# Decoder step with sparse and forgetting heads: two buffers for the compression's prompt rows, both turns behind the second group's loads, and products with cached value pages given out a little later

## The chip, the cores and the metric

The kernel runs on one core of one Trainium2 chip. A core has a matrix engine (TensorE, PE in the profile, with its weight loads as PEld), a vector engine (VectorE, DVE), a scalar engine (ScalarE, ACT), a general engine (GpSimd, POOL) and a sync engine (SyncE, SP). Each runs its own list of instructions in order; they meet at semaphores. SP and POOL also give out DMA transfers. The metric is the device time of one execution in microseconds (us); less is better.

## The reference

One layer of a decoder on two groups of tokens that share all weights: a prompt of 512 tokens, and 8 samples of 4 tokens, each with a past of 1024 tokens in a paged cache (8 pages of 128 rows, found through a page table). Model width 2048, 16 heads of width 128, all in float32.

```python
h = rmsnorm(x, norm_in)
q_n, kv_n, g_n, z_n, q_f, k_f, v_f, f_f, z_f = split(h @ w_in)      # 7712 columns
# 8 sparse heads, 2 shared key/value heads
kc = compress(kv_n[0], cmp_pe[0], cmp_w[0])   # blocks of 32 rows -> one row, 32 products of 128x128
vc = compress(kv_n[1], cmp_pe[1], cmp_w[1])
o_n = g0 * attend(q_n, kc, vc) + g1 * attend(q_n, top 16 blocks of 64) + g2 * attend(q_n, window 512)
# 8 forgetting heads
o_f = softmax(q_f k_f^T / sqrt(128) + D[t] - D[s]) v_f,  D = cumsum(log sigmoid(f_f))
y = rmsnorm(x + concat(o_n * silu(z_n), o_f * silu(z_f)) @ w_out, norm_final)
```

For the samples, keys and values of the past come from the caches, so the kernel reads whole pages of `cache_nsa_kv` and `cache_fox_kv`, and the window from `state_nsa_win`. The compression works on the prompt's rows and on the cached rows of all samples. The new keys, values and log forget values, and the window moved on, are outputs too.

## The kernel before

**A planner writes the order.** The kernel is a Python program that gives out instructions once. A model of the chip (`Clock`, `note` at L105) keeps a time for each engine and DMA queue. The input projection runs as 61 tiles of 128 columns (`run_tiles`, L519): each of four chunks of a tile is 24 matmuls of 272 columns into `pz` (three products for each pair of 128x272 blocks: high by high, high by low, low by high part). Between these matmuls, `S.pump` (L223) lets generators go on that do all other work. A generator yields what it waits for: a list of tiles (until the model has them ready), flags, or a test. `S.after(us)` (L270) is a test that holds until the model's PE clock has gone that far. None of these becomes an instruction; they only move what the generator gives out next, in the order of every engine. The real waits are semaphores that follow the data. All engine calls go through one helper, so that the profile has the line L169 for all, and work is told apart by the names of tiles.

**Weights.** A chunk's weights (`raw`, five buffers, 256 KB from SP) are split into a high part on ACT (`whi`) and a low part on DVE (`wlo`), two chunks ahead of the products (`w_dma` L469, `w_split` L494).

**Compression** (`compress`, L1246). For keys and values (kv = 0 and 1) it first needs the prompt's rows of the tiles c00 and c01, and of c10 and c11. They have just been stored by `store_natural` (L731), which raises the flags nkv00 to nkv11. Eight loads on SP bring the rows of one kv back as `cz`, 64 KB each, in runs of 512 bytes; DVE turns them into `more`, 8 us on the planner's clock after `cz` is ready there. Then come 64 steps with rows gathered from the cache (`crow`, POOL), ending in the results `vt`, `kc_scr` and `vc_scr`.

**The sparse chain** (`nsa`, L2087) runs compression, the prompt's sparse heads (`nsa_prompt`, two halves, the second waits for the flags nkv31 and nkv51 among others) and the samples' sparse heads (`nsa_sample`, L1553). The last has, for each of two groups of four samples, six pairs of value pages: `set_in` (L1569) keeps five page buffers `spg` filled, half of the pages through SP and half through POOL, and `values` (L1806) gives 16 matmuls into `acc` for each pair of two. When this chain ends the flag mx is raised, and the mixing begins.

**The forgetting chain** (`fox`, L2102) runs twice, for four heads each: samples (`fox_sample`, L1084), then prompt (`fox_prompt`, last step `fot`). In the samples' value part a step takes two pages `fpg` of four samples each (eight loads of 256 KB, half on SP and half on POOL), 16 matmuls into `accv`, and asks for the next pages behind them (`ahead`, L1092, two buffers). There are 8 steps in each half, 16 in all.

**The end.** `mix` (L1852) loads for each of 16 heads the gate (`mx`) and the result (`oz`) and multiplies them on DVE; `turn_in` (L1868) splits that into `h_hi` and `h_lo`, and `run_outputs` (L593) multiplies with `w_out` into `po`, head after head.

Of the kernel before, what the change touches and what calls it, by code (L numbers as in the profile page):

```python
# [8 lines left out]
F32 = mybir.dt.float32  # L9
# [6 lines left out]
P = 128  # L16
# [283 lines left out]
def dram(ap, offset, dims):  # L300
    return bass.AP(tensor=ap.tensor, offset=ap.offset + offset, ap=dims)
# [3 lines left out]
def trunk_step(ctx, tc, x_prompt, x_sample, cache_nsa_kv, cache_fox_kv, cache_fox_logf, state_nsa_win,  # L305
# [25 lines left out]
    S = Streams(clock)  # L331
# [44 lines left out]
    def tr_tile(shape, name="tr"):  # L376
        return psum.tile(shape, F32, name=name, tag="tr", bufs=2)
# [4 lines left out]
    def cp(out, in_, scale=1.0):  # L382
        nc.scalar.activation(out, in_, AF.Copy, scale=scale)
# [19 lines left out]
    def mm(out, a, b, start=True, stop=True):  # L403
        nc.tensor.matmul(out, a, b, start=start, stop=stop, skip_group_check=True)
# [361 lines left out]
    def post_qn(h):  # L766
        def f(zt):
            nc.sync.dma_start(z_scr[h], zt)
            flags.add(f"nq{h}")
            yield  # L770
        return f
# [23 lines left out]
    def post_vf(h):  # L795
        def f(zt):
            yield from store_natural(zt, *dst_fox(h, 1), True, f"v{h}")
        return f
# [72 lines left out]
    def load(t, src):  # L871
        nc.sync.dma_start(t, src)
        return t
# [210 lines left out]
    def fox_sample(hh):  # L1084
# [7 lines left out]
        def ahead():  # L1092
            while at[0] < min(len(seq), at[1] + FPG):
                kv, bq, kb = seq[at[0]]
                pages[at[0]] = pg = fx.tile([P, 4, 512], F32, name="fpg", bufs=FPG)
                for b in range(4):
                    if kv:
                        load_page(pg[:, b], cache_fox_kv, (bq * 4 + b) * 8 + kb,
                                  lambda c: c[0, :, 1, hs, :].rearrange("p h d -> p (h d)"))
                    else:  # L1100
                        gather(pg[:, b], dram(cache_fox_kv, 0, [[512, n_pool * 512], [1, 512]]),
                               IX["f"][hh][:, bq * 8 + kb, b:b + 1])
                at[0] += 1
# [100 lines left out]
        for bq in range(2):  # L1204
            acc = psum.tile([P, SEQ], F32, name="accv", tag="accv", bufs=1)
            for kp in range(4):
                pgs = [pages.pop(at[1] + x) for x in range(2)]
                yield [*pgs, pt, acc]
                for x in range(2):
                    kb = kp * 2 + x  # L1210
                    for b in range(4):
                        o = kb * P + (bq * 4 + b) * 16
                        mm(acc[b * 32:b * 32 + 32], pt[:, o:o + 32], pgs[x][:, b], kb == 0, kb == 7)
                at[1] += 2
                yield
                ahead()
            ob = obs[bq]
            cp(ob, acc)
            yield
            yield from S.take()  # L1220
            tp = tr_tile([P, 4, P])
            for g in range(4):
                nc.tensor.transpose(tp[:, g, :], ob[:, g * P:(g + 1) * P], ident)
            yield
            for g in range(4):
                nc.vector.tensor_copy(o_s[:, 8 + hh * 4 + g, bq * 16:bq * 16 + 16].rearrange("p (b t) -> p b t", t=4),
                                      tp[:, g, :].rearrange("p (b r) -> p b r", r=32)[:, :, g * 4:g * 4 + 4])
            S.put()
# [17 lines left out]
    def compress(pl):  # L1246
# [17 lines left out]
        def load_w(s):  # L1264
            if s < 32:
                cg, kv, dp = s // 4, s // 2 % 2, s % 2
                cw[s] = t = pl.tile([P, 2, P], F32, name="cw", bufs=3)
                for d in range(2):
                    load(t[:, d], dram(cmp_w, (kv * 32 + cg * 4) * P * P + (dp * 2 + d) * 32 * P, [[P * P, 4], [P, 32], [1, P]]))
        load_rows(0)  # L1270
        load_w(0)
        load_w(1)
        more = []
        for kv in range(2):
            yield (f"nkv{kv}0", f"nkv{kv}1")
            yield [dram(nsa_kv_prompt, kv * 256 + v * P, [[1024, SEQ], [1, P]]) for v in range(2)]
            cz = pl.tile([P, 8, P], F32, name="cz")
            for c in range(4):
                for v in range(2):
                    load(cz[c * 32 + v * 16:c * 32 + v * 16 + 16],  # L1280
                         dram(nsa_kv_prompt, kv * 256 + v * P + c * 1024, [[32 * 1024, 16], [4 * 1024, 8], [1, P]]))
            yield [cz]
            yield S.after(8.0)
            m = pl.tile([P, 32, MORE], F32, name=f"more{kv}")
            more.append(m)
            nc.vector.memset(m[:, :, 33:], 0.0)
            nc.vector.tensor_copy(m.rearrange("p (g d) k -> p g d k", d=4)[:, :, :, 32],
                                  peT[:, :, kv * 8:kv * 8 + 8].rearrange("p d g -> p g d"))
            nc.vector.transpose(m[:, :, :32], cz.rearrange("p g d -> p (g d)"))
            yield  # L1290
# [12 lines left out]
        for step in steps + [None]:  # L1303
            if step:
                cg, bh, kv, dp = step
# [6 lines left out]
                n = 256 if bh else WIDE  # L1312
# [19 lines left out]
        for kv in range(2):  # L1332
            bc = pl.tile([P, 1], F32, name="bc", bufs=2)
            nc.vector.tensor_copy(bc, pss[kv][:, 288:289])
            pc = pl.tile([P, 32], F32, name="pc", bufs=2)
            nc.vector.tensor_scalar(pc, pss[kv][:, 256:288], bc, None, op0=OP.add)
            vt = pl.tile([P, 2, 8, 32], F32, name="vt", bufs=2)
            for bh in range(2):
                src = (psb[:, kv] if bh else pss[kv][:, :256]).rearrange("p (b v n) -> p v b n", b=4, v=2)
                for v in range(2):  # L1340
                    nc.scalar.activation(vt[:, v, bh * 4:bh * 4 + 4], src[:, v], AF.Identity, bias=bc)
            yield
            vf = vt.rearrange("p v b n -> p v (b n)")
            if kv == 0:
                nc.sync.dma_start(kp_scr, pc)
                nc.sync.dma_start(kc_scr, vf)
            else:
                yield from S.take(2)
                tp = tr_tile([P, 2, 256])
                for grp in range(2):  # L1350
                    for v in range(2):
                        nc.tensor.transpose(tp[:, grp, v * P:(v + 1) * P], vf[:, v, grp * P:(grp + 1) * P], ident)
                tq = tr_tile([16, 2, P])
                for v in range(2):
                    nc.tensor.transpose(tq[:, v, :], pc[:, v * 16:(v + 1) * 16], ident)
                yield
                vn = pl.tile([P, 2, 256], F32, name="crow", bufs=2)
                cp(vn, tp)
                vq = pl.tile([P, 2, P], F32, name="cw", bufs=3)[:16]
                cp(vq, tq)  # L1360
                S.put(2)
                yield
                nc.sync.dma_start(vc_scr, vn)
                nc.sync.dma_start(vp_scr, vq)
# [188 lines left out]
    def nsa_sample(pl):  # L1553
# [82 lines left out]
        for grp in range(2):  # L1636
# [14 lines left out]
            for x in range(2):  # L1651
                a, b = slice(64 * x, 64 * x + 64), slice(64 - 64 * x, 128 - 64 * x)
# [66 lines left out]
            for br in range(2):  # L1719
# [34 lines left out]
                p = T("sp", [P, 1024 + 64]) if br == 0 else p  # L1754
# [51 lines left out]
            def values(k, srcs, n=P, first=False, last=False):  # L1806
                for bb in range(4):
                    mm(acc[bb * 32:bb * 32 + 32], PT[:n, k, bb * 32:bb * 32 + 32], srcs[bb], first, last)
            yield [acc, PT]
            for k in range(0, 12, 2):  # L1810
                ts = [got.pop(0) for _ in range(2)]
                yield ts + [vc] * (k == 8)
                if k == 8:
                    values(12, [vs] * 4, 64)
                    values(13, [vc[:, grp, :]] * 4)
                for x in range(2):
                    values(k + x, [ts[x][:, bb] for bb in range(4)], first=k + x == 0, last=k + x == 11)
                yield ts
                set_in()
                set_in()  # L1820
# [82 lines left out]
    def add_in(col, post):  # L1903
        add_tile(w_in2, [(col, P, 0)], post)
# [3 lines left out]
                 n=lambda h, _: add_in(C_QN + h * P, post_qn(h)),  # L1908
                 q=lambda h, _: add_in(C_QF + h * P, post_qf(h)),
                 k=lambda h, _: add_in(C_KF + h * P, post_kf(h)),  # L1910
                 v=lambda h, _: add_in(C_VF + h * P, post_vf(h)),
# [243 lines left out]
```

## Time and profile before

| what | value |
|---|---|
| median of 3 runs | 1295.4 us (1294.78 to 1297.54) |
| profiled execution, its own time | 1292.8 us |
| its span, first to last instruction | 1291.1 us |
| mean granted clock of TensorE | 0.993 |
| DMA | 266.86 MB, mean 207 GB/s |

The page of the profile gives the busy time of each engine, the span in 40 slices, the DMA queues, the chain of work that ended last, and the costliest groups. The views used further on are the waits (who waited for whom: total, times, longest), the timeline (start, length, engine, line, operation, out<-in, in brackets the idle time before and what ended it), the table by windows (busy time and instructions of each engine in a stretch, the granted clock of PE, the busy share of the DMA engines, GB/s) and the groups of one tile. Times of the trace are of the one profiled execution. Matmuls overlap: the length of one is longer than the step to the next, so a start is the safer thing to read.

### The profile page before, as it was taken

What the parts mean: (1) busy time and instruction counts of PE and PEld (TensorE: products, weight loads), DVE (VectorE), ACT (ScalarE), POOL (GpSimd) and SP (SyncE); (2) the same over time, 40 slices, a digit from 0 to 9 for tenths busy, and PEclk for the clock granted to TensorE, in tenths of its full rate; (3) what the DMA queues carried; (4) which work ended last, traced back from release to release, by engine and by line L of the source; (5) the groups of instructions that cost most, each with busy time, mean ns of one, the idle gap of its engine ahead of it and who ended that gap; (6) DMA issues with size and microseconds to landing.
All of it is one profiled execution on the core that took longest, in us unless ns stands there. A gap on an engine that the chain in (4) does not pass through costs nothing.

```text
span 1291.1 us, 27195 instructions
## 1 busy us (share of the span) xinstructions
PE 1254.9 (97%) x10071; PEld 1130.4 (88%) x10071; DVE 784.5 (61%) x1978; ACT 549.8 (43%) x1193; POOL 284.5 (22%) x376
## 2 busy tenths in 40 slices
PE   8989999999999999999999999899999999999997
PEld 6989999998789999999998888688889988777786
DVE  6735888885546667655687753386566537354255
ACT  5313333434334677652345452256754524333221
POOL 5221277753410000005445012211111200000000
PEclk9989999999999999999999999999999999999999
DMA  7476699998986455659967688977788697334323
GB/s 214 129 192 170 178 279 298 299 288 272 295 272 160 121 157 155 174 157 292 294 199 235 174 239 244 257 211 198 217 233 202 196 304 258 100 114 147 127 76 139
DMA packets 308398, 266.86 MB, mean 207 GB/s; under 512 B 87198, under 2 KB 255150, under 8 KB 307592
## 3 DMA queue, kind: packets, MB, share of 16 engines
q1 hardware_dynamic: 284312, 189.15, 51.4%
q0 software_dynamic: 23904, 75.84, 18.3%
q8 instruction: 79, 1.29, 0.4%
q14 instruction: 55, 0.45, 0.1%
q10 hardware_dynamic: 48, 0.13, 0.0%
HBM read 236.32 MB, written 37.05 MB: 212 GB/s over the span
## 4 chain that ended last, share of the span: by engine, by line
PE 73%; DMA 10%; issue 9%; POOL 2%; DVE 2%; SPq 2%; ACT 2%; POOLq 0%; DVEq 0%; ACTq 0%
PE pz L169 40%; PE po L169 15%; DMA fpg<-in_cache_fox_kv 4%; PE tr L169 4%; PE accv L169 4%; PE s L169 4%; PE acc L169 3%; SPq L169 2%; DMA spg<-in_cache_nsa_kv 1%; POOL crow L169 1%; PE psb L169 1%; DMA spg<-in_state_nsa_win 1%; PE accf L169 1%; DMA xt<-in_x_prompt 1%; POOL fpg L169 1%
## 5 line engine op out<-in xcount | busy, mean ns | idle before, releaser
L169 PE MATMUL pz<-h_hi,whi 128*128 128x272 f32 x1920 | 565.6, 295 | 2.2 <-DVE zt L169 1.6
L169 PE MATMUL pz<-h_hi,wlo 128*128 128x272 f32 x1920 | 554.9, 289 | 5.8 <-DVE wlo L169 5.8
L169 PE MATMUL pz<-h_lo,whi 128*128 128x272 f32 x1920 | 554.4, 289 | 0.0
L169 PEld LDWEIGHTS pz<-h_hi,whi 128*128 128x128 f32 x1920 | 363.4, 189 | 18.2 <-issue 13.6
L169 PEld LDWEIGHTS pz<-h_hi,wlo 128*128 128x128 f32 x1920 | 362.8, 189 | 6.0 <-DVE wlo L169 6.0
L169 PEld LDWEIGHTS pz<-h_lo,whi 128*128 128x128 f32 x1920 | 363.3, 189 | 0.8
L169 DVE TENSOR_TENSOR wlo<-raw,whi 128x512 fp32r<-128x512 f32 x275 | 186.0, 678 | 157.7 <-ACT whi L169 152.9
L169 ACT ACTIVATE whi<-raw 128x512 fp32r<-128x512 f32 x275 | 171.5, 625 | 210.4 <-PE pz L169 96.9
L169 POOL DMA_INDIRECT fpg<-in_cache_fox_kv,fi x128 | 131.6, 1028 | 300.4 <-ACT whi L169 209.7
L169 PE MATMUL po<-whi,h_hi 128*128 128x512 f32 (+1 forms) x256 | 95.5, 373 | 0.0
L169 POOL DMA_INDIRECT crow<-in_cache_nsa_kv,ci x64 | 66.0, 1031 | 125.6 <-DVE ct L169 71.8
L169 PE MATMUL po<-whi,h_lo 128*128 128x512 f32 (+1 forms) x256 | 93.4, 365 | 0.0
L169 PE MATMUL po<-wlo,h_hi 128*128 128x512 f32 (+1 forms) x256 | 93.4, 365 | 0.0
L169 DVE STREAM_TRANSPOSE ft<-fpg 128x1024 f32<-128x1024 f32 x64 | 78.9, 1235 | 17.3 <-DMA fpg<-in_cache_fox_kv,fi 13.2
L169 ACT ACTIVATE cxh<-ct 128x580 fp32r<-128x580 f32 (+1 forms) x64 | 42.2, 660 | 85.1 <-DVE ct L169 75.2
L169 DVE TENSOR_TENSOR zt<-pz,rsb 128x272 f32<-128x272 f32 x56 | 24.6, 439 | 85.3 <-PE pz L169 85.3
L169 POOL DMA_DIRECT2D spg<-in_cache_nsa_kv x64 | 35.0, 546 | 185.3 <-DVE skt L169 57.6
L169 ACT ACTIVATE zt<-pz 128x272 f32<-128x272 f32 x66 | 26.2, 398 | 98.7 <-PE pz L169 98.5
L169 PEld LDWEIGHTS po<-whi,h_hi 128*128 128x128 f32 x256 | 48.1, 188 | 19.7 <-ACT whi L169 7.5
L169 POOL DMA_DIRECT2D fpg<-in_cache_fox_kv x64 | 34.8, 544 | 133.8 <-PE accv L169 96.0
L169 DVE TENSOR_TENSOR cxl<-ct,cxh 128x580 fp32r<-128x580 f32 (+1 forms) x64 | 46.1, 720 | 19.4 <-ACT cxh L169 18.6
L169 PEld LDWEIGHTS po<-whi,h_lo 128*128 128x128 f32 x256 | 48.2, 188 | 8.5
(409 smaller groups left out, 1907.1 us busy)
## 6 DMA issues: line engine op xcount, KB each, us to landing
raw<-in_w_in SPq DMA_DIRECT2D x240, 256.0 KB
fpg<-in_cache_fox_kv POOLq DMA_DIRECT2D x64, 256.0 KB, 7.0
fpg<-in_cache_fox_kv SPq DMA_DIRECT2D x64, 256.0 KB
raw<-in_w_out SPq DMA_DIRECT2D x40, 256.0 KB
spg<-in_cache_nsa_kv POOLq DMA_DIRECT2D x64, 128.0 KB, 5.4
spg<-in_cache_nsa_kv SPq DMA_DIRECT2D x64, 128.0 KB
out<-in_state_nsa_win SPq DMA_DIRECT2D x32, 254.0 KB
scr_z<-zt SPq DMA_DIRECT2D x28, 272.0 KB
```

The source lines that it names most:

```text
L169: return fn(*a, **k)
```

## The change

It has two parts.

In `compress`, the loop over kv is cut in two. The first loop waits for the flags, takes a buffer `cz` and gives out its eight loads; `cz` now has two buffers. The second loop does the two turns into `more`, each 8 us after the buffer is ready on the planner's clock. `vt` at the end takes the two slots of `cz` in place of its own.

In `fox_sample` and in `nsa_sample`, each step of products with value pages yields `S.after(1.5)` once the planner has the pages ready: 16 steps into `accv`, 12 into `acc`.

```diff
@@ fox_sample @@
                 pgs = [pages.pop(at[1] + x) for x in range(2)]
                 yield [*pgs, pt, acc]
+                yield S.after(1.5)
                 for x in range(2):
@@ compress @@
-        more = []
+        more, czs = [], []
         for kv in range(2):
             yield (f"nkv{kv}0", f"nkv{kv}1")
             yield [dram(nsa_kv_prompt, kv * 256 + v * P, [[1024, SEQ], [1, P]]) for v in range(2)]
-            cz = pl.tile([P, 8, P], F32, name="cz")
+            czs.append(pl.tile([P, 8, P], F32, name="cz", bufs=2))
             for c in range(4):
                 for v in range(2):
-                    load(cz[c * 32 + v * 16:c * 32 + v * 16 + 16],
+                    load(czs[kv][c * 32 + v * 16:c * 32 + v * 16 + 16],
                          dram(nsa_kv_prompt, kv * 256 + v * P + c * 1024, [[32 * 1024, 16], [4 * 1024, 8], [1, P]]))
+        for kv, cz in enumerate(czs):
             yield [cz]
             yield S.after(8.0)
             m = pl.tile([P, 32, MORE], F32, name=f"more{kv}")
...
-            vt = pl.tile([P, 2, 8, 32], F32, name="vt", bufs=2)
+            vt = pl.tile([P, 8, P], F32, name="cz", bufs=2)[:, :4].rearrange("p (v b) (c n) -> p v (b c) n", v=2, n=32)
@@ nsa_sample @@
                 ts = [got.pop(0) for _ in range(2)]
                 yield ts + [vc] * (k == 8)
+                yield S.after(1.5)
                 if k == 8:
```

## The prediction

> **What bounds the kernel now.** I read the page first, then the waits of PE, then the timelines around each wait, and the last stage.
>
> ```profile
> span 1291.1 us, 27195 instructions
> ...
> PE 1254.9 (97%) x10071; PEld 1130.4 (88%) x10071; DVE 784.5 (61%) x1978; ACT 549.8 (43%) x1193; POOL 284.5 (22%) x376
> ```
>
> PE works for 97% of the span, so only the 36 us in which it is idle, and slow matmuls, can be won. The waits of PE (total, times, longest) say where the idle time lies:
>
> ```profile
> PE pz L169 <- DVE wlo L169: 5.8, 1, 5.8
> PE accv L169 <- DMA fpg<-in_cache_fox_kv: 5.2, 6, 1.5
> ...
> PE acc L169 <- DMA spg<-in_state_nsa_win: 2.1, 1, 2.1
> PE pz L169 <- DVE zt L169: 1.6, 1, 1.6
> ```
>
> The first three are the places that the diff touches; of the waits it doesn't touch, the longest after the start-up is 1.6 us. The program is emitted by a planner, and each engine then runs its instructions strictly in that order. So a wait on PE is an instruction that the planner put too early, and the cure for it is to put other PE work ahead of it.
>
> **The first wait.** DVE, PE and SP around 80 us (start, length, in brackets the idle time before and its cause):
>
> ```profile
> 79.68 1.25 DVE L169 STREAM_TRANSPOSE more<-cz 128x1024 f32<-128x1024 f32 x1 [8.10 <-DMA cz<-out]
> 80.85 0.65 DVE L169 TENSOR_TENSOR wlo<-raw,whi 128x512 fp32r<-128x512 f32 x1
> ...
> 111.55 1.24 DVE L169 STREAM_TRANSPOSE more<-cz 128x1024 f32<-128x1024 f32 x1
> ```
> ```profile
> 75.47 0.29 PE L169 MATMUL pz<-h_lo,whi 128*128 128x272 f32 x1
> 81.55 0.60 PE L169 MATMUL pz<-h_hi,wlo 128*128 128x272 f32 x1 [5.80 <-DVE wlo L169]
> ```
> ```profile
> 68.82 5.75 SPq L169 DMA_DIRECT2D cz<-out  x8
> 74.67 0.53 SPq L169 DMA_DIRECT2D raw<-in_w_in  x1
> ...
> 97.36 7.07 SPq L169 DMA_DIRECT2D cz<-out  x8
> ```
> ```profile
> 82.00:84.00 2.00, 2.00 (x11) 2.00 (x11) 1.80 (x3) 0.00 (x0) 0.00 (x0) 0.50 1.03 328
> 84.00:86.00 2.00, 2.00 (x13) 2.00 (x13) 0.00 (x0) 0.00 (x0) 0.00 (x0) 0.71 0.52 131
> 86.00:88.00 2.00, 2.00 (x18) 2.00 (x17) 0.69 (x1) 0.63 (x1) 0.00 (x0) 1.00 0.79 136
> ```
>
> DVE stood 8.1 us before the first turn of prompt rows (more<-cz), because SP had issued the loads only from 68.82 to 74.57. Behind it in DVE's order lay the low weight part (wlo) that PE needed next. The second turn, at 111.55, has no bracket: it waited for nothing. In the windows (PE busy and matmuls, PEld, DVE, ACT, POOL, granted clock, DMA share, GB/s) the clock after the gap is 0.50, and 11 and 13 matmuls run in 2 us where 18 do at full clock.
>
> **The turns: what the change does.** It takes away no instruction. One copy, one memset and one transposition of 1.25 us on DVE leave the place at 71 us and come out with the second group, once that group's loads are issued, plus 8 us on the planner's PE clock. They cross no DMA: the second group's eight loads are held by the flags of the tiles c10 and c11, not by the first turn, and keep their place on SP. The second turn then comes 0 to 8 us later on the planner's clock than before, as its 8 us run after the first turn's. The first gathers and products behind it come as much later. By the time of the new first turn the rows of the first group have lain in SBUF for some 20 us, so it waits for nothing; the second keeps its distance to loads that are 7 us earlier like all else. The buffers cost no wait: vt's two slots are cz's, long read by then.
>
> Gain: PE's gap from 75.47 to 81.55 less one normal step of 0.125 us (2 us over 16, two of the 18 only overlapping the edge) is 5.95 us; the half clock lost (18-11) + (18-13) = 12 matmuls, 1.5 us. Together **7.4 us**. What is late next is the raw weights: the load issued at 74.67 stays there, behind cz in the same queue. cz landed at 79.68; 256 KB at the 328 GB/s of the window is 0.8 us more, and two parts of some 0.65 us make it ready near 82.0. PE, no longer stopped, needs it three chunks of 24 matmuls (3.0 us each) after 75.6, at 84.6. So 2.6 us to spare. Low end of this gain: 3 us, if that load is as late again.
>
> **Pages of the forgetting heads.** Sixteen steps of 16 matmuls; an undisturbed one lasts 1.92 us. Five were visibly cut up:
>
> ```profile
> 297.36 1.92 PE L169 MATMUL accv<-fpg,fpt 128*32 128x512 f32 x16
> 308.69 1.91 PE L169 MATMUL accv<-fpg,fpt 128*32 128x512 f32 x12
> 311.34 1.05 PE L169 MATMUL accv<-fpg,fpt 128*32 128x512 f32 x4 [0.74 <-DMA fpg<-in_cache_fox_kv]
> ...
> 333.54 1.24 PE L169 MATMUL accv<-fpg,fpt 128*32 128x512 f32 x8
> ...
> 337.38 1.05 PE L169 MATMUL accv<-fpg,fpt 128*32 128x512 f32 x4 [0.76 <-DMA fpg<-in_cache_fox_kv]
> ...
> 784.73 1.05 PE L169 MATMUL accv<-fpg,fpt 128*32 128x512 f32 x4
> 785.98 2.54 PE L169 MATMUL accv<-fpg,fpt 128*32 128x512 f32 x12 [0.20 <-DMA fpg<-in_cache_fox_kv]
> ...
> 808.14 1.05 PE L169 MATMUL accv<-fpg,fpt 128*32 128x512 f32 x4
> 810.65 2.47 PE L169 MATMUL accv<-fpg,fpt 128*32 128x512 f32 x12 [1.46 <-DMA fpg<-in_cache_fox_kv]
> ...
> 828.17 2.78 PE L169 MATMUL accv<-fpg,fpt 128*32 128x512 f32 x16 [1.27 <-DMA fpg<-in_cache_fox_kv]
> ```
>
> From first start to last end less 1.92: 1.78, 2.97, 1.87, 3.06 and, with the wait ahead of it, 2.13: 11.8 us, twice what the bracketed waits say, since short gaps between groups of four aren't listed. The added S.after(1.5) is no wait on an engine; it lets the planner put 1.5 us of projection matmuls (12) ahead of each step. All five are later than 1.5 us, so each gives back 1.5: **7.5 us**. Bounds: nothing, if the pages follow the products and come late by as much again; 11.8, if fewer transfers at once also make them faster. The next pages are asked for after the step, so they too come 1.5 us later; as the lateness is counted from that point, I take 7.5.
>
> **Pages of the sample's sparse heads.** Twelve steps, normally 1.07 us each:
>
> ```profile
> 925.13 1.07 PE L169 MATMUL acc<-spg,PT 128*32 128x256 f32 x16
> ...
> 946.04 0.64 PE L169 MATMUL acc<-spg,PT 128*32 128x256 f32 x8
> 948.75 1.08 PE L169 MATMUL acc<-spg,PT 128*32 128x256 f32 x8 [2.07 <-DMA spg<-in_state_nsa_win]
> ```
> ```profile
> 812.00:816.00 4.00, 4.00 (x31) 3.09 (x28) 0.00 (x0) 0.00 (x0) 3.35 (x7) 1.00 0.97 218
> ...
> 950.00:952.00 2.00, 2.00 (x10) 2.00 (x11) 0.43 (x2) 0.91 (x4) 0.55 (x1) 0.50 1.11 283
> ```
>
> One step lost 3.79 - 1.07 = 2.7 us, and the clock fell to 0.50 behind it: 8 matmuls fewer in 2 us, 1.0 us. I take 1.5 of the wait and the 1.0: **2.5 us**, between 0 and 3.7. [...]
>
> **What the delays cost.** 16 x 1.5 = 24 us longer for the forgetting heads, 12 x 1.5 = 18 us at most for the sparse heads' sample part. PE has projection matmuls to fill these, as long as some are left:
>
> ```profile
> 557.53 0.39 SPq L169 DMA_DIRECT2D scr_o<-not  x1
> ...
> 593.98 1.55 SPq L169 DMA_DIRECT2D vcz<-scr_vp  x2
> ```
> ```profile
> L169 ACT ACTIVATE fot<-accf x16: 365/383/387, 476.4 to 976.0; 128x256 f32<-128x256 f32 x16
> ```
> ```profile
> 1051.57 0.42 SPq L169 DMA_DIRECT2D mx<-scr_m  x1
> ```
> ```profile
> 1059.02 0.68 DVE L169 TENSOR_TENSOR mx<-mx,oz 128x512 f32<-128x512 f32 x1
> ...
> 1089.67 1.28 DVE L169 TENSOR_TENSOR mx<-mx,oz 128x512 f32<-128x512 f32 x2
> ```
> ```profile
> 1051.11 31.57 PE pz L169 x252
> 1082.68 198.87 PE po L169 x1152
> ```
>
> The prompt's sparse chain ends its first half at 557.53 and starts the second at 593.98, as it waits for the flags of tiles c31 and c51: 36 us that swallow the later compression (8 us) and the first half of the forgetting heads' delay. The forgetting heads end at 976 and would end near 1000, ahead of the sample part's end at 1051.57. That end is what counts: there the mixing starts, its first product at 1059.02, and PE needs head 0 when po starts at 1082.68. With the product and two more passes of about 0.65 us, some 2 us, there are 21 us of slack. The later heads follow every 2.0 us (15 in 30.7 us) and po takes 12 matmuls of 512 columns for each, over 2.5 us, so head 0 decides. 18 us fit in 21: no cost, with little to spare.
>
> The new order also redraws the small waits that nothing here aims at. They may go (-5) or come (+9, six of the 1.5 us kind, since the second half's value steps now run into the sample part's page loads). I take +2, one of the size of the untouched row of 1.6 us and some.
>
> **The sum.** -7.4 - 7.5 - 2.5 + 2.0 = -15.4 us. The profiled execution took 1292.8 us for its span of 1291.1; it becomes 1277.4. The median of the three runs, 1295.4, lies 2.6 above it, so I forecast **1280.0**.
>
> **Rivals.** (1) The delayed products gain nothing, because pages are asked for later by the same 1.5 us: for this, each step's loads do follow the last step; against, steps that were on time lie between late ones. 1280.0 + 7.5 + 2.5 = 1290. Chance 0.15. (2) The raw weights take the place of the turn, 3.0 us and the half clock's 1.5 again: 1284.5; for it, cz and raw share SP's queue; against, 2.6 us to spare. 0.10. (3) The turn doesn't come clear of its loads, the second waits as the first did: 1287.4; against, its row without a bracket. 0.07. (4) The half clock at 950 has another cause than the wait ahead of it and stays, 1.0 us: 1281.0; for it, the clock was whole from 812 to 816, behind the wait of 1.46 us; against, its row stands right behind the wait. 0.05. [...] (5) Slower: the delays add up along one chain, as both chains share the page buffers' queues on SP and POOL, and reach the mixing: 24 + 18 + 2 = 44 us against 21. From 21 us on each one costs PE a microsecond, from 36 the gain is gone; at 44 it is 1303. For it: fewer than 32 us of pure projection are left; against, the gap at 557 to 594 and the end at 976. 0.08. The forecast, 1273 to 1287, has 0.55.
>
> **Chances and range.** A measurement of this kernel tells some 0.2% (2.6 us) from no change. Faster than 1292.8: the forecast, (2), (3), (4) and 0.09 of (1): 0.86; within: 0.06 of (1); slower: 0.08. The range 1271 to 1291 takes in the forecast's, (2) to (4) and most of (1), and leaves out (5), the rest of (1) and the best ends of all terms together (1267).
>
> **What would show it.** Right: no bracket before either more<-cz, clock 1.00 from 70 to 95; steps of accv with at most 1.6 us lost, and later spaced; acc<-spg without the half clock; mx loads nearer to po, and po without a gap. Wrong: a PE wait for wlo or raw near 84; accv steps that lose as much as before; pz run out before the first mx product.

## The result, and the profile after

| kernel | median | runs | ratio to before, 95% interval |
|---|---|---|---|
| before | 1295.6 us | 18 (1289.3 to 1298.8) | 1 |
| after | 1301.9 us | 18 (1299.6 to 1306.0) | 1.0054 [1.0041, 1.0067] |

The change made the kernel slower by 6.3 us. The forecast was 1280.0 us, with a range of 1271 to 1291; the measured time lies outside it, on the other side of the kernel before. The profiled execution of after took 1301.87 us by its own time, 9.1 more than that of before, and lies at the median.

The page of after (busy time of each engine), and behind it its waits of PE (total, times, longest):

```profile
span 1299.9 us, 27179 instructions
...
PE 1255.8 (97%) x10071; PEld 1131.0 (87%) x10071; DVE 785.5 (60%) x1978; ACT 547.6 (42%) x1187; POOL 285.6 (22%) x376
```
```profile
PE pz L169 <- DVE zt L169: 11.3, 3, 6.1
PE s L169 <- DMA kvc<-scr_kc: 5.0, 1, 5.0
PE tr L169 <- DMA fqb<-out: 4.8, 1, 4.8
PE tr L169 <- ACT fp L169: 3.5, 3, 2.2
...
PE pz L169 <- DVE wlo L169: 1.8, 3, 1.0
```

All three waits that the change aimed at are gone from the head of this list: wlo fell from 5.8 to 1.8 us, `spg` no longer stands in it, and `fpg` fell from 5.2 to 0.5. Three waits of 5 to 6 us stand there, for `zt`, `kvc` and `fqb`; before had none of that length for these. PE runs the same 10071 matmuls, and the loss is idle time and the half clock around it. The busy time is only 0.9 us more because two things offset each other in it: matmuls at half clock take longer (in after 10 and 11 in 2 us at 0.50 from 874 to 880, 18 at 1.00 from 90 to 94), and the value steps of the forgetting heads, whose short gaps count as busy (that of before at 828.17 is busy for all its 2.78 us), are cut up less (counted as in the prediction they lose 7.0 us in after, 12.2 in before).

**The start went about as forecast.** The two turns on DVE, the split of two late weight loads on ACT, the first wait of PE that follows, and one window over the place, of before and of after (PE busy and matmuls, PEld, DVE, ACT, POOL, granted clock, DMA share, GB/s):

```profile
101.70 1.24 DVE L169 STREAM_TRANSPOSE more<-cz 128x1024 f32<-128x1024 f32 x1
...
112.92 1.24 DVE L169 STREAM_TRANSPOSE more<-cz 128x1024 f32<-128x1024 f32 x1
```
```profile
82.91 0.63 ACT L169 ACTIVATE whi<-raw 128x512 fp32r<-128x512 f32 x1 [5.78 <-DMA raw<-in_w_in]
...
87.83 0.63 ACT L169 ACTIVATE whi<-raw 128x512 fp32r<-128x512 f32 x1 [4.28 <-DMA raw<-in_w_in]
```
```profile
89.59 0.40 PE L169 MATMUL pz<-h_hi,whi 128*128 128x272 f32 x1 [2.47 <-DVE zt L169]
```
```profile
70.00:96.00 26.00, 20.20 (x149) 19.98 (x148) 8.35 (x16) 5.20 (x9) 7.54 (x8) 0.87 0.75 196
```
```profile
70.00:96.00 26.00, 23.53 (x189) 23.31 (x189) 8.42 (x14) 5.54 (x9) 7.88 (x8) 1.00 0.88 223
```

Neither turn waits, and the clock is whole. Idle time in these 26 us fell from 5.80 to 2.47 us, and the half clock, 0.13 of 26 us = 3.4 us at the granted 0.87, is gone: 6.7 us in the measure of lost time used from here on. This measure counts half clock inside a gap twice. In windows of 0.5 us the clock of before is 0.50 from 78.5 us on, some 3 us ahead of the gap's end at 81.55, which is 1.6 of the 3.4 us; so what PE won at the start is nearer 5 us. What is left is rival (2) in small: the weights are the next to be late, with the loads split at 82.91 and 87.83.

**The loss stands at one place.** The same view from 800 to 890 us, before and after:

```profile
800.00:890.00 90.00, 80.84 (x693) 71.82 (x692) 51.80 (x170) 38.09 (x72) 13.29 (x25) 0.98 0.91 237
```
```profile
800.00:890.00 90.00, 72.97 (x592) 59.23 (x592) 43.74 (x130) 26.12 (x45) 14.42 (x27) 0.89 0.89 235
```

I call "lost" the idle time of PE plus 90 us times what the granted clock falls short of 1. Before: 9.2 + 1.8 = 11.0 us. After: 17.0 + 9.9 = 26.9 us. That is 15.9 us more, or some 14 without the half clock inside the gaps (1.6 us of after's 9.9). Less the gain at the start, 5 us in the same counting, 9 us are left, and the profiled executions differ by 9.1. The rest of the span adds up to about nothing, though not because nothing happens there: a wait of 2.74 us at 361.55 with a half clock behind it (last section) stands against the value steps that are cut up less. The DMA engines are no fuller than before (0.89 against 0.91).

**What PE does there.** The timeline of PE in after, then DVE's and SP's ahead of the waits:

```profile
803.59 2.92 PE L169 MATMUL accv<-fpg,fpt 128*32 128x512 f32 x16 [0.52 <-DMA fpg<-in_cache_fox_kv]
...
824.70 2.08 PE L169 MATMUL s<-kvc,qv 128*128 128x256 f32 x4 [5.05 <-DMA kvc<-scr_kc]
...
826.71 3.14 PE L169 MATMUL accv<-fpg,fpt 128*32 128x512 f32 x16
...
839.28 1.92 PE L169 MATMUL accv<-fpg,fpt 128*32 128x512 f32 x16
...
857.49 0.57 PE L169 MATMUL pz<-h_hi,whi 128*128 128x272 f32 x1 [6.10 <-DVE zt L169]
...
859.12 3.64 PE L169 MATMUL accv<-fpg,fpt 128*32 128x512 f32 x16
...
873.45 0.91 PE L169 MATMUL tr<-fpn,fqb 32*128 32x32 f32 x4 [4.80 <-DMA fqb<-out]
```
```profile
855.17 1.25 DVE L169 STREAM_TRANSPOSE skt<-spg 128x1024 f32<-128x1024 f32 x1 [3.64 <-DMA spg<-in_cache_nsa_kv]
...
856.91 0.43 DVE L169 TENSOR_TENSOR zt<-pz,rsb 128x272 f32<-128x272 f32 x1
```
```profile
809.35 2.62 SPq L169 DMA_DIRECT2D spg<-in_cache_nsa_kv  x2
...
816.73 2.36 SPq L169 DMA_DIRECT2D fpg<-in_cache_fox_kv  x4
819.14 0.85 SPq L169 DMA_DIRECT2D kvc<-scr_kc  x1
...
868.86 0.72 SPq L169 DMA_DIRECT2D fqb<-out  x1
```

The samples' sparse part begins (`s<-kvc`) while three value steps of the forgetting heads are still to come. Its page loads and theirs alternate on SP, and `kvc` lies behind both; `fqb`, issued at 868.86, lies behind page loads of the sparse part (855.11 to 867.51). On DVE, `zt`, which PE's projection needs, lies behind turns of `skt` that wait for pages (3.64 us ahead of 855.17). Whether the pages are late because both kinds share the DMA engines, or because of the order in which SP and POOL give them out, no run separates. Before, the order was another: the last value step began at 828.17 (the row is in the prediction), and the samples' sparse part behind it:

```profile
842.91 1.88 PE L169 MATMUL s<-kvc,qv 128*128 128x256 f32 x4
```

**Why the two parts meet.** Three starts on SP tell it: the second half of the prompt's sparse heads (`vcz`), that of the forgetting heads (`fss`), and the first load of the samples' sparse part, behind the end of the prompt's sparse heads (`skt`). Before (vcz at 593.98 stands in the prediction), then after:

```profile
588.89 0.63 SPq L169 DMA_DIRECT2D fss<-scr_f  x1
...
802.89 0.49 SPq L169 DMA_DIRECT2D skt<-scr_c  x1
```
```profile
586.32 1.52 SPq L169 DMA_DIRECT2D vcz<-scr_vp  x2
...
594.86 0.62 SPq L169 DMA_DIRECT2D fss<-scr_f  x1
...
779.94 0.57 SPq L169 DMA_DIRECT2D skt<-scr_c  x1
```

The starts moved by only 6 to 8 us, but they changed places. I read the rest so: the half that goes first in the planner's round is served first from there on. The prompt's sparse heads end 23 us earlier (skt), the forgetting heads' value steps later (last one 828 to 859). So 23 us one way and 31 the other bring two parts together that had followed one another. Not all of the 31 is the order: with the turns alone (e1 below), where the value steps have no delay, `skt` is 22 us earlier (780.49) and the last value step 14 us later (842.06).

### The profile page after: what moved, and what is told of

Read it like the earlier page. It is cut to its first block, busy times and chain, and to the rows that moved or that the text cites. A ratio compares the mean times of both kernels' runs of the same rounds, so it can differ in the third digit from the quotient of the medians.

```text
span 1299.9 us, 27179 instructions
## 1 busy us (share of the span) xinstructions
PE 1255.8 (97%) x10071; PEld 1131.0 (87%) x10071; DVE 785.5 (60%) x1978; ACT 547.6 (42%) x1187; POOL 285.6 (22%) x376
## 4 chain that ended last, share of the span: by engine, by line
PE 81%; DMA 9%; SPq 3%; DVE 3%; ACT 2%; issue 2%; POOL 1%; DVEq 0%; ACTq 0%
PE pz L169 46%; PE po L169 15%; PE s L169 5%; PE tr L169 5%; PE accv L169 4%; PE acc L169 3%; SPq L169 3%; PE psb L169 2%; DMA fpg<-in_cache_fox_kv 1%; DMA spg<-in_cache_nsa_kv 1%; DMA raw<-in_w_in 1%; PE accf L169 1%; DMA spg<-in_state_nsa_win 1%; DMA cw<-in_cmp_w 1%; DMA dsb<-scr_d 1%
## 5 line engine op out<-in xcount | busy, mean ns | idle before, releaser
L169 PE MATMUL pz<-h_hi,whi 128*128 128x272 f32 x1920 | 565.5, 295 | 11.3 <-DVE zt L169 11.3
L169 DVE TENSOR_TENSOR zt<-pz,rsb 128x272 f32<-128x272 f32 x62 | 27.2, 438 | 75.3 <-PE pz L169 75.1
```

The costliest lines, as they stand in the source:

```text
L169: return fn(*a, **k)
```

## The experiments

Two theories were to be told apart at first. **Overlap:** the loss comes from the samples' sparse part running beside the last value steps of the forgetting heads. **Redraw:** any other order deals out other small waits, and this one happened to be bad. "Late end" joined them as a third: what is put off ends later.

"Lost" in the table is worked out as above, from the window 800 to 890 of each kernel's profile. "Beside" says whether the samples' sparse part begins ahead of the last value step. Executions of one kernel differ by up to some 13 us (and one of e12's took 3576 us) and each profile is one of them, so the medians give the size and the profiles the place. Each ratio is to the kernel before in the same batch.

| kernel | median, runs | ratio to before | beside | lost |
|---|---|---|---|---|
| before | 1295.3 to 1295.7 | 1 | no | 11.0 |
| after | 1301.9, 18 | 1.0054 [1.0041, 1.0067] | yes | 26.9 |
| e1 turns | 1302.2, 8 | 1.0049 [1.0032, 1.0066] | yes | 24.5 |
| e2 accv | 1304.3, 6 | 1.0081 [1.0062, 1.0101] | yes | 23.4 |
| e3 acc | 1289.2, 5 | 0.9950 [0.9935, 0.9965] | no | 8.5 |
| e4 turns, acc | 1298.8, 12 | 1.0019 [1.0002, 1.0036] | yes | 26.9 |
| e5 turns, old order | 1291.6, 12 | 0.9969 [0.9950, 0.9987] | no | 12.6 |
| e6 before, 14 us | 1311.6, 6 | 1.0133 [1.0100, 1.0166] | yes | 20.4 |
| e7 before, 8 us | 1299.2, 12 | 1.0031 [1.0011, 1.0050] | no | 14.9 |
| e8 turns, acc, old order | 1284.4, 6 | 0.9921 [0.9896, 0.9947] | no | 12.0 |
| e9 e6 with hold | 1301.0, 12 | 1.0044 [1.0028, 1.0059] | no | 10.2 |
| e10 after with hold | 1290.7, 12 | 0.9960 [0.9939, 0.9981] | no | 14.5 |
| e11 after, old order, hold | 1293.9, 12 | 0.9996 [0.9978, 1.0014] | no | 14.6 |
| e12 e8 with accv in half 1 | 1291.0, 12 | 0.9959 [0.9941, 0.9978] | no | 12.2 |
| e13 e8 with accv in half 2, hold | 1289.4, 8 | 0.9955 [0.9938, 0.9971] | no | 14.0 |
| e14 accv, old order, hold | 1291.8, 12 | 0.9965 [0.9950, 0.9981] | no | 12.7 |
| e15 e13 without hold | 1297.5, 12 | 1.0016 [1.0000, 1.0033] | yes | 20.5 |

All kernels with "yes" lost 20 to 27 us in this stretch, all with "no" 8 to 15. The half clock inside gaps, which is counted twice, makes up to 3 us of it (e2); without it the two groups are 19 to 26 and 8 to 14.

**e1 to e4: the parts alone.** e1 takes the two hunks in `compress` alone, e2 the line in `fox_sample`, e3 the line in `nsa_sample`, e4 e1 and e3 together. The diffs from here on are cut to the changed lines and a few around them.

```diff
  e1: the hunks of compress (czs, vt)
  e2: fox_sample
                 yield [*pgs, pt, acc]
+                yield S.after(1.5)
  e3: nsa_sample
                 yield ts + [vc] * (k == 8)
+                yield S.after(1.5)
  e4: e1 and e3
```

> Only the two turns are moved; no later products. Overlap theory (the later forgetting steps make the loss, as their page loads then run beside those of the samples' sparse heads): the gap before wlo goes, some 2.5 us come back as a wait for raw weights near 88, the waits after 800 us look as in the kernel before; time 4 to 6 us below it, about 1290. Redraw theory (any new order draws new waits, whatever part makes it): a wait of 3 us or more appears somewhere that the kernel before has none, and the time lies anywhere from 1288 to 1302.

> Only the 16 steps of the forgetting heads' value pages come 1.5 us later; turns as before. Overlap theory: the gap at 75 to 81 us is back; the steps into accv lose under 5 us in all where they lost 11.8; waits for kvc, fqb and zt of 4 us or more after 800 us are there; time 5 to 13 us above the kernel before, about 1304. Redraw theory: no such group of waits after 800 us has to be there; time anywhere from 1290 to 1304.

> Only the 12 steps of the samples' sparse value pages come 1.5 us later. Nothing before 925 us changes in either theory. Overlap theory: the wait of 2.1 us at 948 and the half clock behind it go, the end of the sparse chain stays ahead of the end of the projection: time 2 to 4 us below the kernel before, about 1292.5. Redraw theory: the waits after 925 us are drawn anew, within 3 us to either side.

> The change without the forgetting heads' part. Overlap theory: the two gains add, 6 to 9 us below the kernel before, about 1288; no wait of 4 us or more on PE after 800 us. Redraw theory: gains need not add; time anywhere from 1285 to 1302, and the waits after 800 us differ from those of the run with the turns alone.

Measured: 1302.2, 1304.3, 1289.2 and 1298.8 us. The turns alone and the forgetting heads' delay alone each make the kernel as slow as the whole change, or slower. In both, `vcz` goes ahead of `fss` (585.46 and 594.19 in e1, 589.37 and 597.96 in e2). The sparse delay alone leaves the old order and is faster by 6 us. So the parts don't add; what e1, e2 and e4 share with after is the order. The overlap theory, as it was written for these runs, blamed the later value steps and expected 1290 for e1 and 1288 for e4. Both missed by more than 10 us, since the turns alone bring the overlap too. In e2 the value steps were to lose under 5 us in all; they lose 9.6, all in the second half.

**e5 and e8: the old order given back.** The forgetting heads raise a flag when they begin a half, and the prompt's sparse heads wait for it, as they wait for the projections. e5 has that with the turns, e8 with the turns and the sparse delay.

```diff
 fox_sample
         ahead()
+        flags.add(f"foxgo{hh}")
 nsa_prompt and nsa
-                yield (f"nkv3{kvh}", f"nkv5{kvh}")
+                yield (f"nkv3{kvh}", f"nkv5{kvh}", f"foxgo{kvh}")
-            yield ("compress", "gf") + tuple(f"nkv{s}{kvh}" for s in range(2, 6))
+            yield ("compress", "gf", f"foxgo{kvh}") + tuple(f"nkv{s}{kvh}" for s in range(2, 6))
```

> The turns alone, and the prompt's sparse second half waits in the planner until the forgetting heads' second half has started, as it did in the kernel before. In the order of PE the samples' sparse part (first product with kvc) then stands behind the eighth value step again, where the turns alone put it ahead of the seventh. Overlap theory (the loss comes from the samples' sparse page loads running beside the last value steps): no PE wait of 3 us or more after 300 us, time 4 to 6 us below the kernel before, about 1290. Theory that the moved turns cost by themselves, or that any new order does: 1298 to 1304 as with the turns alone.

> The turns and the later sparse value pages, with the second halves started in the order of the kernel before; the forgetting heads' value steps as before. Overlap theory: the gains add, some 5 us from the turns and some 6 us from the sparse value pages: about 1285. Other theories: no better than the sparse value pages alone, 1289.

Measured: 1291.6 against 1302.2 for e1, and 1284.4 against 1298.8 for e4. The same parts, 10.6 and 14.4 us faster. The window 800 to 890 of e1, e5 and e8:

```profile
800.00:890.00 90.00, 77.22 (x605) 64.70 (x604) 45.72 (x125) 30.09 (x53) 14.84 (x28) 0.87 0.90 236
```
```profile
800.00:890.00 90.00, 82.81 (x684) 72.62 (x683) 49.31 (x160) 39.03 (x72) 9.67 (x18) 0.94 0.87 215
```
```profile
800.00:890.00 90.00, 81.65 (x701) 72.46 (x700) 53.02 (x166) 41.87 (x77) 10.50 (x20) 0.96 0.89 225
```

From e1 to e5 11.9 us of lost time go, from e4 to e8 14.9; the medians fell by 10.6 and 14.4. e8 is the fastest kernel of the study.

**e6 and e7: the loss without the change.** The kernel before, with nothing but a pause ahead of the forgetting heads' second half: 14 us in e6 (the diff), enough for the parts to run beside each other in the planner's order, 8 us in e7, not quite enough.

```diff
 fox
                 if hh:
+                    yield S.after(14.0)
                     yield gate("right")
```

> The kernel before with one line: the forgetting heads' second half starts 14 us later on the planner's clock. No turn is moved and no product given out later. PE's order then has the samples' sparse part ahead of the seventh value step, as with the turns alone. Overlap theory: waits of PE of 3 us or more on fpg, kvc, skt or sp between 800 and 880 us, the gap before wlo near 81 as before; time 4 to 10 us above the kernel before, about 1302. Other theories: within 3 us of it.

> As the run with 14 us, with 8 us: the order then keeps the samples' sparse part behind all value steps. Overlap theory: within 3 us of the kernel before. A theory by which a later second half costs in proportion to its delay: some 4 us above it, if 14 us cost 7.

Measured: 1311.6 and 1299.2. With 14 us the old kernel loses 16 us, with 8 us 3.5, more than the overlap theory expected of either (4 to 10, and 3 at most); the step between them comes with the overlap. In both the second halves change places (`vcz` at 593.50 and `fss` at 604.86 in e6, 593.21 and 598.31 in e7), but only in e6 do the parts meet, so the order alone is not the loss. Part of both numbers is a stop of PE that the pause itself brings, and that before doesn't have: 4.67 us at 609.44 in e6, 3.02 at 602.70 in e7. These two runs alone would also fit the late end.

**e9 and e10: only the overlap taken away.** The samples' sparse part waits until the sixth of the eight value steps has been given out; e9 does that in e6, e10 in the changed kernel. No other line is changed, and the sparse part ends later for it.

```diff
 fox_sample
                 at[1] += 2
+                if bq * 4 + kp == 5:
+                    flags.add(f"foxv{hh}")
                 yield
                 ahead()
 nsa_sample
-        yield ("compress", "gf") + tuple(f"nq{h}" for h in range(8)) + tuple(
+        yield ("compress", "gf", "foxv1") + tuple(f"nq{h}" for h in range(8)) + tuple(
```

> The kernel before, with 14 us put ahead of the forgetting heads' second half (as in e6, which gave 1311.6 us) and, beside it, the samples' sparse part held until the sixth of the eight value steps of that half has been given out, so that its page loads no longer run beside them. Overlap theory (the loss comes from page loads of two kinds running at once): the loss of e6 goes, 1294 to 1301 us, and the waits and half-clock stretches between 800 and 890 us are about those of before. Theory of redrawn waits (any other order costs about this much): 1306 us or more. Late-end theory (what costs is that the last part comes later): 1311 us or more, since holding it makes it later still.

> The whole change (1301.9 us) and, beside it, only the hold of e9: the samples' sparse part waits for the sixth value step of the forgetting heads' second half. Overlap theory: the parts' gains come through, 1283 to 1292 us. Theory of redrawn waits: 1298 us or more. Late-end theory: the samples' part starts some 15 us later than in the changed kernel and eats the slack before the mixing; the time stays at 1298 us or above with a wait of 5 us or more in front of the last rows.

Measured: 1301.0, at the edge of what overlap gives, and 1290.7, inside it. e9 is 10.6 us faster than e6, e10 11.2 us faster than the changed kernel. The window of e6, e9 and e10 (for after see above):

```profile
800.00:890.00 90.00, 79.47 (x618) 65.29 (x617) 42.56 (x138) 27.06 (x46) 14.28 (x26) 0.89 0.93 238
```
```profile
800.00:890.00 90.00, 81.63 (x683) 69.41 (x681) 45.87 (x150) 29.57 (x55) 15.99 (x29) 0.98 0.96 238
```
```profile
800.00:890.00 90.00, 79.15 (x607) 66.67 (x600) 42.74 (x141) 28.21 (x51) 15.41 (x28) 0.96 0.88 231
```

Lost time falls by 10.2 us from e6 to e9 and by 12.4 from after to e10, again what the medians show. Redraw and late end both expected 1298 us or more for e10, and late end 1311 for e9: both fall. What e9 keeps above before, 5 us, isn't in this stretch; it has the stop that the pause brings, as e6 and e7 do:

```profile
609.39 0.47 PE L169 MATMUL pz<-h_hi,wlo 128*128 128x272 f32 x1 [4.08 <-DVE wlo L169]
```

**e11 and e12: the forgetting heads' delay on top of e8.** e11 is the whole change with the old order and the hold; e12 is e8 with that delay in the first half alone (`if hh == 0`).

> The whole change, with the old order of the two second halves given back (the sparse one may not begin before the forgetting one, as in e8) and the hold of e9. e8 is this without the 1.5 us ahead of the forgetting heads' value products, and took 1284.4 us. If that part of the change saves the stops at its pages (about 5 us of the 11.8 us of waits that the kernel before has there): 1278 to 1282 us. If it saves nothing: 1283 to 1287 us. If the later products push the end back: 1289 us or more.

> As e8 (both turns together, the sparse value products later, the old order of the two second halves; 1284.4 us), with the 1.5 us ahead of the forgetting heads' value products in the first half alone, where no page loads of another part can run beside them later. If the stops at the value pages of the first half are worth their length (some 5 us in the kernel before): 1279 to 1282 us. If they are given back elsewhere: 1283 to 1287 us.

Measured: 1293.9 and 1291.0. The delay that was to save 5 us or so costs 9.5 on top of e8 (with the hold beside it), and 6.6 with the first half alone; e8 was measured on another chip. e12 lies above both of its expectations. e11 lies where its third one had it, but not by a later end: from 1060 us on PE is idle for 9.4 us in e11 and 9.6 in e8. Nor is it the overlap, as e11 and e12 lose no more than 2.6 us over e8 between 800 and 890. More of it lies ahead of 400 us, where PE is idle for 14.6 us in e11, 10.1 in e12 and 7.8 in e8.

**e13 to e15: that delay by itself.** e13 is e8 with the delay in the second half alone and the hold, e14 the kernel before with the delay in both halves, the old order and the hold; e15 is e13 without the hold, so that the sparse part begins one value step earlier.

```diff
  e13, e15: fox_sample, with e8's lines (e15 without the hold)
                 yield [*pgs, pt, acc]
+                if hh == 1:
+                    yield S.after(1.5)
  e14: as e2, with the lines foxgo and foxv1, without turns and sparse delay
```

> As e8 (both turns together, the sparse value products later, old order of the two second halves; 1284.4 us), with the 1.5 us ahead of the forgetting heads' value products in the second half alone and the samples' sparse part held behind the sixth of them. e12 has the first half alone (1291.0), e11 both (1293.9). If each half costs its own amount: 1285 to 1290 us. If the second half's delay saves the stops at its pages: 1279 to 1283 us. If the cost comes from the later end that any delay there brings: 1291 us or more.

> The kernel before with the delay of the forgetting heads' value products alone (both halves), the old order of the two second halves and the hold, so that nothing of the turns, of the sparse value products or of the overlap is in it; before 1295.7 us. If the delay gives what the prediction's sum has: 1286 to 1291 us. If it gives nothing because the pages come later with the products: 1293 to 1298 us. If it costs what e11 shows against e8 (9.5 us): 1301 to 1308 us.

> e13 without the hold: only the start of the samples' sparse part moves, to ahead of the last of the forgetting heads' eight value steps in place of behind it. Overlap theory: 3 to 8 us more than e13, with a stop or a half clock at the last value step or at the first sparse products behind it. Theory of redrawn waits or of the end: the time of e13 within 2 us, or less, as the samples' part starts earlier.

Measured: 1289.4, 1291.8 and 1297.5. e14: with the old order and without the turns, the delay gains 3.5 us, between "nothing" and the 7.5 of the sum. Counted as in the prediction (each of the 16 steps from first start to last end less 1.92 us, with the wait ahead of it), the steps lose 12.2 us in before and 8.4 in e14: 3.8 less, as the time says. All of that is won in the first half, where they lose nothing in place of 5.1; in the second they lose 8.4 in place of 7.1. e15 against e13 is the narrowest test of the overlap: one step of it costs 8.0 us in the medians. Its profiled execution (1292.0 by its own time) lies 5.4 us below its median, yet it shows two of the stops of the changed kernel at their length there; e13 has none for `fqb`, and 2.5 us as its longest for `zt`. PE in e15:

```profile
846.12 1.88 PE L169 MATMUL tr<-fpn,fqb 32*128 32x32 f32 x8 [5.14 <-DMA fqb<-out]
...
864.87 0.56 PE L169 MATMUL pz<-h_hi,whi 128*128 128x272 f32 x1 [5.49 <-DVE zt L169]
```

**e16 to e18: e8, e11 and e13 together.**

> The kernel of e8 once more, beside e11's and e13's kernels on one chip, because e8 (1284.4 us), e11 (1293.9) and e13 (1289.4) were measured on three. Its median falls within 1282 to 1288 us if e8's was no lucky draw.

> The kernel of e11 beside e16. If the delay of the forgetting heads' value products really costs some 9 us on top of the turns and the later sparse products: 7 us or more above e16. If the difference lay in the chips: within 3 us of e16. If it saves what it saved alone (3.5 us in e14): below e16.

> The kernel of e13 (the delay in the second half alone) beside e16. A real cost of the second half: 3 us or more above e16; chips: within 2 us of it.

Here everything took longer, the kernel before 1361.4 us (19 runs), so e16's range of 1282 to 1288 can't be used, and only the kernels of this batch are compared with one another: 1348.0 (6 runs), 1356.4 (12) and 1348.3 (8), or 0.9906 [0.9876, 0.9936], 0.9966 [0.9942, 0.9990] and 0.9916 [0.9887, 0.9946] of before. The whole delay costs 8.4 us over e8's kernel, as e11 said (9.5). The second half alone costs 0.3, so e13's 5.0 was not confirmed. That leaves the first half, which e12 had alone, as the one that costs; e12 itself was not run again.

## Why the prediction was wrong

**The step that failed: "What the delays cost".** It took each chain by itself. "36 us that swallow the later compression (8 us) and the first half of the forgetting heads' delay" is true for the sparse chain's end, but the other chain starts at 588.89, within 5.1 us of 593.98. The shifts of 6 and 8 us were enough to change the places of the two starts. From that came the overlap: 22 us the one way and 14 the other with the turns alone, 23 and 31 with the delays. e5 and e8, which give back only the order, and e9 and e10, which take away only the overlap, each recover 10 to 14 us. e9 and e10 keep the two starts in the changed order, so what costs is the overlap, and the order only brings it about.

**The term that was mis-sized: "The new order also redraws the small waits ... I take +2".** The overlap had been seen, "since the second half's value steps now run into the sample part's page loads", but it was priced as six waits of 1.5 us and then taken at 2. It measured 15.9 us of lost time, some 14 without what is counted twice: three waits of 5 to 6 us, where the profile shows pages ahead of what PE waited for, on SP ahead of `kvc` and `fqb`, issued at 819.14 and 868.86 and waited for until 824.70 and 873.45, and on DVE, which stood 3.64 us for `spg`, ahead of `zt`, and about 7 us of half clock behind them (0.50 from 824 to 828, 858 to 862 and 874 to 880). This was a mechanism with a place, and not noise around zero.

**The turns, -7.4.** Right in place, and about 5 us of the 7.4 came at the start (6.7 in lost time, with half clock counted twice); the 2.47 us that came back are the difference. Alone in the old order they give 4.0 us in the medians (e5). "2.6 us to spare" for the raw weights held for the load it named, split at 82.91; the next one made the wait of 2.47 us. Rival (3) didn't happen; rival (2) came at about half its price, 2.47 of 4.5 us, without the half clock.

**Value pages of the forgetting heads, -7.5.** The sum added it to the turns' gain. By itself it is worth 3.5 us (e14). With the turns in place it costs 8.4 to 9.5 (e11, e17), nearly all of it in the first half. One reason can be read from the steps: with the turns together and without this delay, the first half's eight steps lose 2.1 us in e8, where before had 5.1. Most of what the delay was to win there had gone already. That the delay then makes new stops is seen in after, in a wait for `zt` at 361.55 with a half clock behind it (below) that e8 lacks. It stands, with 2.3 to 2.7 us, in all four kernels that have both the turns and the delay in the first half (after, e10, e11, e12), and is 0.5 us at most (e5) in those of e1 to e15 that have only one of them; in after, ACT had stood 4.26 us ahead of it for weights of the compression (`cw`). It is less than half of the cost in e11 and e12, and the rest stays open. Rival (1), no gain because pages are asked for later, is thus half right.

**Value pages of the sparse heads, -2.5.** The stop is gone in after and in e3 (neither has a wait of PE for `spg` in its list), and in after the clock is 1.00 from 890 to 1060, where before had 0.50 from 949 to 952, so rival (4) did not happen. e3 gains 6.1 us in the medians, and 3.0 by the two profiled executions, mostly since that of before lies 2.8 us below its median. By the medians 2.5 and its upper bound of 3.7 were too low; by the profiles it is nearly right.

**Rival (5)** gave a time, 1303, close to the result, but by luck: its mechanism did not happen. It had the delays reach the mixing; but the gates of head 0 are loaded at 1050.64, and from 1060 us on PE has no gap:

```profile
1050.64 0.43 SPq L169 DMA_DIRECT2D mx<-scr_m  x1
```
```profile
1060.00:1280.00 220.00, 220.00 (x1283) 1.00 0.41 136
```

**What adds up.** With the old order, the turns give 4.0 us (e5) and the sparse delay 6.1 (e3), together 10.1; e8, which has both, measures 11.3 below before.

**The signs** that were to show the prediction right came true at the turns (no bracket, clock 1.00 from 70 to 96), at the sparse value pages and nearly at the value steps of the forgetting heads (at most 1.72 us lost, where 1.6 was set), and the time was still wrong: none of them asks what the moved parts then run beside.

## What to carry to other kernels

In a program whose order is written by a planner, look for the places where two independent chains start close together, and ask of each shift, however small, whether it makes them change places; here 5 us of distance decided over 10 to 14. A delay that costs nothing in its own chain has to be followed into what it then runs beside, and a part that shares queues with it, as the two here share SP (the loads of `spg` at 809.35 and of `fpg` at 816.73), is the first to look at. Gains at several stops need not add: measure each one on top of the others, and in the order that the final kernel will have.

## What the runs showed of the hardware

A half clock followed some waits of PE and not others of nearly the same length. In after, the wait of 2.74 us ahead of 361.55 was followed by it (11 matmuls in 2 us at 0.50), the wait of 2.47 us at 89.59 was not (clock 1.00 in its window above). At the place of the first, 2.31 us ahead of 363.47 in e12 were not: the next products into `pz` start 0.12 to 0.20 us apart, where in after they start 0.22 to 0.33 us apart. PE's row, then the windows of PE (busy and matmuls, granted clock, DMA share, GB/s):

```profile
361.55 0.54 PE L169 MATMUL pz<-h_hi,whi 128*128 128x272 f32 x1 [2.74 <-DVE zt L169]
```
```profile
360.00:362.00 2.00, 0.45 (x2) 0.90 0.58 145
362.00:364.00 2.00, 2.00 (x11) 0.50 0.30 100
```

In after, the waits of 5.05, 6.10 and 4.80 us were followed by it too (0.50 from 824 to 828, 858 to 862 and 874 to 880). In before, 2.07 us ahead of 948.75 were followed by it (0.50 from 950 to 952), and 1.46 us ahead of 810.65 were not (1.00 from 812 to 816; both windows are in the prediction). So some waits of 2.07 us and more cost this kernel more than their length, and the length alone does not tell which.

The last batch took 5% longer throughout (before: 1361.4 in place of 1295.6; the same chip had given 1295.7 for it in the batch of e9 to e12). Ratios to before moved by at most 0.4%, and e11's kernel stayed the slowest of the three. In the profile of e16 the longest group of waits is one that the profile gives no releaser for; its cause stays open:

```profile
PE pz L169 <- issue: 13.3, 22, 1.8
```
